# A causal way and a full way of attention behind one branch, and rope keys on all 128 rows

## The chip, the core and the metric

The kernel runs on one core of a Trainium2 chip. A core has a matmul engine (TensorE, "PE", with its weight loads as "PEld"), a vector engine (VectorE, "DVE"), an activation engine (ScalarE, "ACT"), GpSimd ("POOL") and SyncE ("SP"), each with an instruction stream of its own. They work on a memory on the chip, matmuls write into an accumulator memory (PSUM), and DMA queues move data from and to device memory. SyncE issues the weight loads, GpSimd most other transfers. The metric is the time of one execution on the device, in microseconds (us).

## What is computed

Three layers over 512 tokens of width 2048, all in fp32. The first is a recurrent mixer (two kinds of linear recurrence, a gate, an output projection, a layer norm). The second is an attention with 16 heads whose queries and keys are made from small inner vectors and have a part of 64 columns turned by position (rope). The third is an attention with 8 heads that subtracts two softmaxes from each other. The change touches only how the two attentions leave out what the mask forbids:

```python
CHUNK, Q_BLOCK, SEQ = 64, 128, 512

def chunk_allowed(pos_q, pos_k):
    return (pos_k // CHUNK)[:, None, :] <= (pos_q // CHUNK)[:, :, None]

def mla_attend(q, k, v, pos):          # second layer, 16 heads, d = 128 + 64
    ...
    sc = jnp.einsum('bhqd,bhkd->bhqk', qi, k_t).astype(jnp.float32) * scale
    sc = jnp.where(chunk_allowed(pi, pos)[:, None], sc, -jnp.inf)
    p = jax.nn.softmax(sc, axis=-1)
    return jnp.einsum('bhqk,bhkd->bhqd', p.astype(v_t.dtype), v_t)

def diff_attend(q, k, v, pos, lam):    # third layer, 8 heads, 2 components, value width 256
    ...
    sc = sc + bias[:, :, None]         # -slope * |distance|
    sc = jnp.where(chunk_allowed(pi, pos)[:, None, None], sc, -jnp.inf)
    p = jax.nn.softmax(sc, axis=-1)
    p_diff = p[:, :, 0] - lam * p[:, :, 1]
    return jnp.einsum('bhqk,bhkd->bhqd', p_diff.astype(v_t.dtype), v_t)

positions = jnp.arange(SEQ)            # an input of the kernel
```

The positions are an input. With positions that count up, a block of 128 queries sees its own block of keys and those before it, and nothing of the blocks behind.

## The kernel before

All activations lie transposed: 128 features on the partitions, 512 tokens along the free dimension. A matmul takes a weight block of 128 × 128 as its stationary operand and 512 columns (tokens) as the moving one. For accuracy each fp32 number is held as a high and a low part (`split`: ScalarE casts the high part, VectorE subtracts it to get the low part), and each product is three matmuls (`mm3`, lines 115 to 117: high × high, low × high, high × low) in a one-pass fp32 format. Weights come in units of 512 KB into three rotating tiles `raw`, and `unit` splits them into `whi` and `wlo`.

Each attention works head by head. `scores(j)` of the second layer makes, for each of 4 blocks `a` of 128 queries, a score tile of 128 × 512 with five matmuls: three for the 128 plain columns, two for the rope (line 572 with the key's high part on 128 rows, line 573 with its low part on the 64 rows of that head). `attention_rows` adds the mask (VectorE, line 316), takes the maximum, and ScalarE makes the exponentials; line 575 scales the rows by their sum. Then `PV` turns the 4 × 4 blocks (`turn`, line 609, one PE transpose each), splits them, and multiplies by the values (`step`). These pieces are hung into the gate's and the next pair's projections by slice number: `pv.at(7, 9, 12, 14)` means that the first turn stands ahead of slice 7 of a projection of 16 slices. The third layer does the same with `scores(a)` (two components, each with a bias tile `bm`) and two value halves.

A scheduler orders each engine's stream from this code; engines then wait for each other through semaphores.

At the start SyncE loads the first weight units and the input slices `f` in turn, ScalarE and VectorE split them, and TensorE begins with the two projections of `proj_side`.

Of the kernel before, what the change touches and what calls it, by code (L numbers as in the profile page):

```python
# [19 lines left out]
T = 512  # L20
# [7 lines left out]
class Core:  # L28
    def __init__(self, ctx, tc):
# [7 lines left out]
        self.hl = ent(tc.tile_pool(name="hl", bufs=1))  # L37
        self.ps = ent(tc.tile_pool(name="ps", bufs=2, space=PSUM))
        self.dr = ent(tc.tile_pool(name="dr", bufs=1, space=DRAM))
        self.ones = self.cp.tile([128, 128], F32, name="ones")  # L40
        nc.vector.memset(self.ones, 1.0)
        self.ones_r = self.cp.tile([128, 128], F32R, name="onesr")
        nc.vector.tensor_copy(self.ones_r, self.ones)
# [4 lines left out]
        self.consts = {}  # L48
        self.ahead = []


    def const_col(self, v):
        if v not in self.consts:
            t = self.cp.tile([128, 1], F32, name=f"c{len(self.consts)}")
            self.nc.vector.memset(t, float(v))
            self.consts[v] = t
        return self.consts[v]
# [35 lines left out]

    def unit(self, src, n):
# [3 lines left out]
        raw = self.wp.tile([128, 1024], F32, tag="raw", name="raw", bufs=3)  # L98
        self.nc.sync.dma_start(raw[:, :n], src)
# [60 lines left out]
    def hl_tiles(self, n=KD):  # L160
        h = [self.hl.tile([128, T], F32R, tag=f"h{i}", name=f"h{i}") for i in range(n)]
        l = [self.hl.tile([128, T], F32R, tag=f"l{i}", name=f"l{i}") for i in range(n)]
        return h, l

# [16 lines left out]
    def token_sums(self, wk, out, sq):  # L181
# [3 lines left out]
        d = wk.tile([128, 128], F32, tag="diag", name="diag", bufs=1)  # L185
        for a in range(4):
            self.nc.vector.tensor_tensor_reduce(out=d, in0=ps[:, a * 128:a * 128 + 128], in1=self.ident, scale=1.0,
                                                scalar=0.0, op0=ALU.mult, op1=ALU.add, accum_out=out[:, a:a + 1])
# [7 lines left out]
    def sigmoid(self, out, x, tmp):  # L196
# [3 lines left out]
        self.act(out, tmp, AF.Exp, scale=-1.0)  # L200

# [108 lines left out]
def attention_rows(co, wk, scores, bias, scale, nb):  # L310
# [3 lines left out]
    p = wk.tile([128, T], F32, tag="p", name="p", bufs=nb)  # L314
# [18 lines left out]
def mla_layer(co, w, tables, enter, after, out):  # L333
# [7 lines left out]
    with ExitStack() as ctx:  # L341
# [133 lines left out]
        for pr in range(8):  # L475
# [38 lines left out]
            kpl = wk.tile([128, T], F32R, tag="kpl", name="kpl", bufs=1)  # L514
# [8 lines left out]
            def k_rms(j):  # L523
# [12 lines left out]
                l = kpl[halves[j], :]  # L536
                co.tt(l, kpf[halves[j], :], h[halves[j], :].bitcast(F32), ALU.subtract)
# [27 lines left out]
            def scores(j):  # L565
                P = []
                hf = halves[j]
# [30 lines left out]
class PV:  # L598


    def __init__(self, co, wk, P, n, vh, vl, off):
# [3 lines left out]
    def turn(self, kt):  # L605
        co = self.co
        pt = co.psum("g")
        for a in range(4):
            co.nc.tensor.transpose(pt[:, a * 128:(a + 1) * 128], self.P[a][:, kt * 128:(kt + 1) * 128], co.ident)  # L609
        h = self.wk.tile([128, T], F32R, tag="pth", name="pth", bufs=2)  # L610
        l = self.wk.tile([128, T], F32R, tag="ptl", name="ptl", bufs=2)
        co.split(h, l, pt)
# [27 lines left out]
class Gated:  # L640
# [3 lines left out]
    def __init__(self, co, name, order=range(KD)):  # L644
# [3 lines left out]
        self.h, self.l = [None] * KD, [None] * KD  # L648

    def hl(self, i):  # L650
        co = self.co
        self.h[i] = co.hl.tile([128, T], F32R, tag=f"h{i}", name=f"h{i}")
        self.l[i] = co.hl.tile([128, T], F32R, tag=f"l{i}", name=f"l{i}")
# [9 lines left out]
    def get(self, first, eng=None):  # L663
# [4 lines left out]
        for u in range(KD // 2 - 1):  # L668
            raw = co.wp.tile([128, 1024], F32, tag="raw", name="raw", bufs=3)
# [1054 lines left out]
```

## Time and profile before

| | |
|---|---|
| Median of 3 runs | 3068.97 us (3066.61 to 3069.67) |
| The profiled execution | 3074.24 us |
| Its span, first to last instruction | 3072.5 us |
| Mean granted TensorE clock | 0.985 of full speed |
| Instructions | 43493 |
| Moved by DMA | 294.41 MB, 96 GB/s |

The profiled execution is a single one, 5.3 us above the median. A span is the time from the first instruction to the last. A matmul's shown duration contains its way through the engine, so the distance from one start to the next is what a matmul costs in a stream.

### The profile page before, as it was taken

Reading aid. Unit: us, or ns where it says so; the run is one execution under the profiler, and the core shown is the slowest. Engines: PE = TensorE matmul, PEld = TensorE weight load, DVE = VectorE, ACT = ScalarE, POOL = GpSimd, SP = SyncE. Lnnn points to the kernel's source line nnn. Section 1 sums busy time; section 2 is a strip of 40 time slices with the busy share of each in tenths; the row PEclk is TensorE's granted clock in tenths of the full one; section 3 lists DMA queues with packets and bytes.
Section 4 is the critical chain, followed back from the end, with each engine's and each line's share of the span. In section 5 each row is a group of like instructions: output and inputs, shape, how many; then the busy total and the mean of one; then the engine's idle time right before and its main releaser. Section 6 shows DMA issues by size and latency. Waiting matters only on the chain.

```text
span 3072.5 us, 43493 instructions
## 1 busy us (share of the span) xinstructions
PE 2995.8 (98%) x16606; PEld 2462.5 (80%) x16606; DVE 1841.7 (60%) x3617; ACT 1442.6 (47%) x2628; POOL 434.9 (14%) x793
## 2 busy tenths in 40 slices
PE   8799999999999899799999999999999999999999
PEld 6687787787787788577777787888888888888887
DVE  6455745647546585948777776346466556655632
ACT  5354545545545432646555665244444444444521
POOL 0312303303213310710000000100000000000000
PEclk9899999999999799899999999999999999999999
DMA  4222222223223343232221124432222222222443
GB/s 172 66 88 75 83 77 81 83 78 85 74 77 90 102 158 124 93 103 69 73 72 63 66 76 158 144 137 83 95 84 76 97 90 83 83 90 90 140 146 112
DMA packets 92033, 294.41 MB, mean 96 GB/s; under 512 B 15232, under 2 KB 15664, under 8 KB 91696
## 3 DMA queue, kind: packets, MB, share of 16 engines
q1 hardware_dynamic: 73984, 246.89, 23.5%
q0 software_dynamic: 17840, 44.74, 5.1%
q8 instruction: 130, 2.13, 0.3%
q14 instruction: 79, 0.65, 0.1%
HBM read 263.95 MB, written 27.53 MB: 95 GB/s over the span
## 4 chain that ended last, share of the span: by engine, by line
PE 62%; DVE 2%; ACT 1%; DMA 1%; issue 1%; POOL 0%; DVEq 0%; ACTq 0%; SPq 0%
PE pj L115 17%; PE pj L117 17%; PE pj L116 17%; PE g L115 2%; PE g L116 2%; PE g L117 2%; PE g L609 1%; PE g L573 1%; PE g L194 1%; PE g L193 1%; PE g L572 0%; DVE t L76 0%; DVE l L73 0%; DVE wlo L73 0%; DMA raw<-og 0%
## 5 line engine op out<-in xcount | busy, mean ns | idle before, releaser
L115 PE MATMUL pj<-h,whi 128*128 128x512 f32 x2848 | 1145.4, 402 | 15.0 <-ACT h L81 14.2
L116 PE MATMUL pj<-l,whi 128*128 128x512 f32 x2848 | 1119.4, 393 | 9.8 <-DVE l L73 9.2
L117 PE MATMUL pj<-h,wlo 128*128 128x512 f32 x2848 | 1119.5, 393 | 4.7 <-DVE wlo L73 4.6
L73 DVE TENSOR_TENSOR wlo<-raw,whi 128x512 fp32r<-128x512 f32 x864 | 601.0, 699 | 767.7 <-ACT whi L81 740.6
L81 ACT CAST whi<-raw 128x512 fp32r<-128x512 f32 x864 | 534.0, 620 | 924.2 <-PE pj L116 778.7
L115 PEld LDWEIGHTS pj<-h,whi 128*128 128x128 f32 x2848 | 538.4, 189 | 137.6 <-ACT h L81 15.9
L117 PEld LDWEIGHTS pj<-h,wlo 128*128 128x128 f32 x2848 | 538.8, 189 | 123.5 <-DVE wlo L73 6.9
L116 PEld LDWEIGHTS pj<-l,whi 128*128 128x128 f32 x2848 | 539.7, 189 | 116.2 <-DVE l L73 11.8
L115 PE MATMUL pj<-whi,h 128*128 128x256 f32 x768 | 221.3, 288 | 0.0
L116 PE MATMUL pj<-wlo,h 128*128 128x256 f32 x768 | 217.2, 283 | 0.0
L117 PE MATMUL pj<-whi,l 128*128 128x256 f32 x768 | 217.1, 283 | 0.0
L115 PEld LDWEIGHTS pj<-whi,h 128*128 128x128 f32 x768 | 147.0, 191 | 4.7 <-issue 1.4
L116 PEld LDWEIGHTS pj<-wlo,h 128*128 128x128 f32 x768 | 147.2, 192 | 1.2
L117 PEld LDWEIGHTS pj<-whi,l 128*128 128x128 f32 x768 | 147.1, 192 | 0.2
L70 ACT ACTIVATE p<-p,mx,rq 128x512 f32<-128x512 f32 x128 | 104.2, 814 | 84.1 <-DVE mx L318 83.7
L73 POOL TENSOR_TENSOR gs<-gs,rs 128x512 f32<-128x512 f32 x16 | 20.4, 1291 | 712.3 <-ACT rs L70 712.3
L73 POOL TENSOR_TENSOR mt<-m,at 128x60 f32<-128x60 f32 (+24 forms) x248 | 93.3, 376 | 92.6 <-DMA at<-d 73.8
L73 POOL TENSOR_TENSOR m<-m,mt 128x60 f32<-128x60 f32 (+24 forms) x248 | 95.4, 385 | 19.4
L73 DVE TENSOR_TENSOR ptl<-g,pth 128x512 fp32r<-128x512 f32 x96 | 65.3, 686 | 52.9 <-ACT pth L81 52.7
L73 DVE TENSOR_TENSOR sql<-sq,sqh 128x512 fp32r<-128x512 f32 x96 | 66.3, 691 | 32.7 <-ACT sqh L81 32.5
L81 ACT CAST pth<-g 128x512 fp32r<-128x512 f32 x96 | 56.2, 586 | 63.2 <-PE g L609 58.5
L81 ACT CAST sqh<-sq 128x512 fp32r<-128x512 f32 x96 | 59.4, 618 | 18.0 <-DVE sq L73 8.9
(440 smaller groups left out, 4015.5 us busy)
## 6 DMA issues: line engine op xcount, KB each, us to landing
raw<-w_in SPq DMA_DIRECT2D x114, 512.0 KB, 3.2
raw<-b_qk SPq DMA_DIRECT2D x64, 512.0 KB, 3.2
raw<-a_in SPq DMA_DIRECT2D x50, 512.0 KB, 3.2
raw<-w_out SPq DMA_DIRECT2D x32, 512.0 KB, 3.3
raw<-a_out SPq DMA_DIRECT2D x32, 512.0 KB, 3.6
raw<-b_v SPq DMA_DIRECT2D x32, 512.0 KB, 3.2
raw<-b_g SPq DMA_DIRECT2D x32, 512.0 KB, 3.2
raw<-b_out SPq DMA_DIRECT2D x32, 512.0 KB, 3.4
```

Source lines behind the costliest of these rows:

```text
L70: self.nc.scalar.activation(out, in_, func, scale=scale, **kw)
L73: return (eng or self.nc.vector).tensor_tensor(out, in0=a, in1=b, op=op)
L81: self.nc.scalar.copy(hi, src)
L115: mm(out, lhsT=ahi, rhs=bhi, start=start, stop=False)
L116: mm(out, lhsT=ahi, rhs=blo, start=False, stop=False)
L117: mm(out, lhsT=alo, rhs=bhi, start=False, stop=stop)
L193: self.nc.tensor.matmul(out, lhsT=ones, rhs=h, start=True, stop=False)
L194: self.nc.tensor.matmul(out, lhsT=ones, rhs=l, start=False, stop=True)
L573: mm(sc, lhsT=qps[j][hf, ts], rhs=kps[j][1], start=False, stop=True)
L609: co.nc.tensor.transpose(pt[:, a * 128:(a + 1) * 128], self.P[a][:, kt * 128:(kt + 1) * 128], co.ident)
```

## The change

The program asks once, on the device, whether every block of 128 positions lies wholly behind the block before it (in chunks of 64), and then runs one of two complete copies of all three layers. In the first copy (`co.causal`), a score tile for query block `a` has only the first 128·(a+1) keys, the turns leave out the blocks above the diagonal, and a value product for key block `kt` covers only the queries from 128·kt on. The second copy computes everything, as before. In both copies the low part of the rope key has 128 rows. Buffers that were handed out by a pool are now fixed tiles, so that both copies use the same ones; the constants are columns of one tile, and the diagonal of the token sums is written back to PSUM in place.

```diff
+        self.raws = [self.wp.tile([128, 1024], F32, name=f"raw{i}", bufs=1) for i in range(3)]
+        self.causal = False
+
+    def span(self, a):
+
+        return a * 128 + 128 if self.causal else T
...
+    def load(self, src):
+
+        if self.loaded:
+            return self.loaded.pop(0)
+        raw = self.raws.pop(0)
+        self.raws.append(raw)
...
+def in_order(co, wk, w):
...
+    row = wk.tile([1, T], I32, name="posrow1")
+    f = row.bitcast(F32)
+    nc.sync.dma_start(row, w["pos"].rearrange("(a t) -> a t", a=1))
+    dve.tensor_scalar(row, row, 6, None, op0=ALU.arith_shift_right)
+    dve.tensor_copy(f, row)
+    hi = wk.tile([1, 8], F32, name="order")
+    lo, flag = hi[:, 4:8], co.cp.tile([1, 1], I32, name="inorder")
+    fb = f.rearrange("p (a t) -> p a t", a=4)
+    dve.tensor_reduce(hi[:, 0:4], fb, axis=AX.X, op=ALU.max)
+    dve.tensor_reduce(lo, fb, axis=AX.X, op=ALU.min)
+    for a in (2, 1):
+        co.tt(lo[:, a:a + 1], lo[:, a:a + 1], lo[:, a + 1:a + 2], ALU.min)
+    co.tt(hi[:, 0:3], lo[:, 1:4], hi[:, 0:3], ALU.is_gt)
+    dve.tensor_reduce(hi[:, 3:4], hi[:, 0:3], axis=AX.X, op=ALU.min)
+    dve.tensor_copy(flag, hi[:, 3:4])
+    return flag
...
-    p = wk.tile([128, T], F32, tag="p", name="p", bufs=nb)
+    p = wk.tile([128, T], F32, tag="p", name="p", bufs=nb)[:, 0:n]
...
-                l = kpl[halves[j], :]
-                co.tt(l, kpf[halves[j], :], h[halves[j], :].bitcast(F32), ALU.subtract)
+                l = wk.tile([128, T], F32R, tag="kpl", name="kpl")
+                co.tt(l, kpf, h.bitcast(F32), ALU.subtract)
...
-                    sc = co.psum("g")
+                    n = co.span(a)
+                    sc = co.psum("g")[:, 0:n]
                     ts = slice(a * 128, a * 128 + 128)
-                    co.mm3(sc, qs[j][0][:, ts], qs[j][1][:, ts], ks[j][0], ks[j][1], True, False)
-                    mm(sc, lhsT=qps[j][:, ts], rhs=kps[j][0], start=False, stop=False)
-                    mm(sc, lhsT=qps[j][hf, ts], rhs=kps[j][1], start=False, stop=True)
-                    p, rs = attention_rows(co, wk, sc, mask[:, a, :], rq[:, j, a:a + 1], 4)
+                    co.mm3(sc, qs[j][0][:, ts], qs[j][1][:, ts], ks[j][0][:, 0:n], ks[j][1][:, 0:n], True, False)
+                    mm(sc, lhsT=qps[j][:, ts], rhs=kps[j][0][:, 0:n], start=False, stop=False)
+                    mm(sc, lhsT=qps[j][:, ts], rhs=kps[j][1][:, 0:n], start=False, stop=True)
+                    p, rs = attention_rows(co, wk, sc, mask[:, a, 0:n], rq[:, j, a:a + 1], 4, n)
...
-        for a in range(4):
+        a0 = kt if co.causal else 0
+        for a in range(a0, 4):
...
+            o = o[:, kt * 128 if self.co.causal else 0:T]
...
+        with tc.tile_pool(name="ord", bufs=1) as wk:
+            ordered = nc.values_load(in_order(co, wk, w), min_val=0, max_val=1)
+        first = [co.load(x) for x in (w["w_in"][32, 0], w["xT"][0:256].rearrange("(a p) t -> p a t", p=128),
+                                      w["w_in"][8, 0])]
+        consts = dict(co.consts)
+
+        with tc.If(ordered > 0) as cmp:
+            co.causal, co.loaded = True, list(first)
+            layers(co, w, out)
+        with cmp.Else():
+            co.causal, co.consts, co.loaded = False, consts, list(first)
+            layers(co, w, out)
```

The third layer's `scores` gets the same `n` for its bias tile, its three matmuls and its softmax.

TensorE, in the middle of the second layer, where the scores of an odd head begin. Names read out<-moving,stationary: `g` is the PSUM score tile, `knh`/`knl` the key's parts, `qnh`/`qnl` the query's, `kph`/`kpl` the rope key's, `qps` the rope query's. Before, the first two of four query blocks:

```order
L115 MATMUL g<-knh,qnh 128x512
L116 MATMUL g<-knl,qnh 128x512
L117 MATMUL g<-knh,qnl 128x512
L572 MATMUL g<-kph,qps_12325 128x512
L573 MATMUL g<-kpl,qps_12325 128x512
L115 MATMUL g<-knh,qnh 128x512
L116 MATMUL g<-knl,qnh 128x512
L117 MATMUL g<-knh,qnl 128x512
L572 MATMUL g<-kph,qps_12325 128x512
L573 MATMUL g<-kpl,qps_12325 128x512
```

The same place in the first copy after:

```order
L136 MATMUL g<-knh,qnh 128x128
L137 MATMUL g<-knl,qnh 128x128
L138 MATMUL g<-knh,qnl 128x128
L610 MATMUL g<-kph,qps_12098 128x128
L611 MATMUL g<-kpl,qps_12098 128x128
L136 MATMUL g<-knh,qnh 128x256
L137 MATMUL g<-knl,qnh 128x256
L138 MATMUL g<-knh,qnl 128x256
L610 MATMUL g<-kph,qps_12098 128x256
L611 MATMUL g<-kpl,qps_12098 128x256
```

The order is the same and the widths are cut; the third and fourth block have 384 and 512 columns.

TensorE, the end of a gate projection of the second layer, where the last turn and the last value products of a head stand (`p` is a softmax row tile, `ident` the identity, `pth`/`ptl` the turned parts, `vh`/`vl` the values). Before:

```order
L609 MATMUL g<-ident,p 128x128 x4
L115 MATMUL pj<-h_11273,whi 128x512
L116 MATMUL pj<-l_11289,whi 128x512
L117 MATMUL pj<-h_11273,wlo 128x512
L115 MATMUL pj<-h_11274,whi 128x512
L116 MATMUL pj<-l_11290,whi 128x512
L117 MATMUL pj<-h_11274,wlo 128x512
L115 MATMUL g<-pth,vh 128x512
L116 MATMUL g<-ptl,vh 128x512
L117 MATMUL g<-pth,vl 128x512
L115 MATMUL g<-pth,vh 128x512
```

After:

```order
L649 MATMUL g<-ident,p 128x128
L136 MATMUL pj<-h_79,whi 128x512
L137 MATMUL pj<-l_95,whi 128x512
L138 MATMUL pj<-h_79,wlo 128x512
L136 MATMUL pj<-h_80,whi 128x512
L137 MATMUL pj<-l_96,whi 128x512
L138 MATMUL pj<-h_80,wlo 128x512
L136 MATMUL g<-pth,vh 128x256
L137 MATMUL g<-ptl,vh 128x256
L138 MATMUL g<-pth,vl 128x256
L136 MATMUL g<-pth,vh 128x128
```

Three of the four last transposes are gone, and the products of the last two key blocks have 256 and 128 columns.

SyncE, at the program's start (`raw` is a weight unit or, after, also the first input slice; `f` the other input slices). Before:

```order
L99 DMA raw<-w_in 128x1024
L728 DMA f<-xT 128x2x512
L99 DMA raw<-w_in 128x1024
L728 DMA f<-xT 128x2x512 x3
L99 DMA raw<-w_in 128x1024
```

After:

```order
L226 DMA posrow_114<-pos 1x512
L113 DMA raw_108<-w_in 128x1024
L111 DMA raw_109<-xT 128x2x512
L113 DMA raw_110<-w_in 128x1024
L740 TENSOR_LOAD inorder
L740 ISA x2
L745 COMPARE_AND_BRANCH
L783 DMA f<-xT 128x2x512 x3
L113 DMA raw_108<-w_in 128x1024
```

The position load stands first, and the reading of the flag and the branch stand between the third big load and the fourth.

## Rows read from the trace of the kernel before

**Rows 1.** The page, part 1: busy time, share of span, instructions.

```profile
PE 2995.8 (98%) x16606; PEld 2462.5 (80%) x16606; DVE 1841.7 (60%) x3617; ACT 1442.6 (47%) x2628; POOL 434.9 (14%) x793
```

**Rows 2.** Busy time by stretch: from:to, length, then engines; clock, DMA share, GB/s.

```profile
36.00:1036.00 1000.00, 959.40 (x6645) 783.23 (x6643) 567.42 (x1007) 487.81 (x886) 260.48 (x582) 0.96 0.26 81
...
1395.00:1900.00 505.00, 504.59 (x2393) 394.55 (x2392) 388.89 (x924) 303.98 (x578) 28.91 (x32) 1.00 0.24 80
...
2180.00:2890.00 710.00, 710.00 (x3809) 613.84 (x3809) 415.97 (x906) 321.50 (x596) 21.68 (x24) 1.00 0.26 90
```

**Rows 3.** Waits: engine and line, whom it waited for, total us, times, longest.

```profile
ACT whi L81 <- PE pj L116: 778.7, 517, 3.1
...
PE g L1334 <- DVE pm L1330: 26.3, 2, 16.9
```

**Rows 4.** Timeline of TensorE, scores of an even head: start, duration, instruction.

```profile
1529.06 0.39 PE L117 MATMUL g<-knh,qnl 128*128 128x512 f32 x1
1529.29 0.40 PE L572 MATMUL g<-kph,qps 128*128 128x512 f32 x1
1529.62 0.50 PE L573 MATMUL g<-kpl,qps 64*128 64x512 f32 x1
1530.05 0.50 PE L115 MATMUL g<-knh,qnh 128*128 128x512 f32 x1
...
1531.60 0.50 PE L115 MATMUL g<-knh,qnh 128*128 128x512 f32 x1
```

**Rows 5.** Timeline of TensorE, matmuls of 256 columns; five lie between.

```profile
1397.77 0.28 PE L115 MATMUL pj<-whi,ckvh 128*128 128x256 f32 x1
...
1398.46 0.28 PE L115 MATMUL pj<-whi,ckvh 128*128 128x256 f32 x1
```

**Rows 6.** Groups by line and form on TensorE: xcount, busy us, mean ns.

```profile
L609 PE MATMUL g<-ident,p 128*128 128x128 f32 x384 | 57.7, 272 | 0.0
...
L573 PE MATMUL g<-kpl,qps 64*128 64x512 f32 x64 | 31.7, 496 | 0.0
```

**Rows 7.** Timeline of TensorE, the first turns of the same head.

```profile
1540.11 0.60 PE L609 MATMUL g<-ident,p 128*128 128x128 f32 x4
...
1540.78 0.40 PE L116 MATMUL pj<-l,whi 128*128 128x512 f32 x1
```

**Rows 8.** Timeline of TensorE, eight passes of 64 columns, one matmul of 512 between.

```profile
207.74 1.00 PE L1521 MATMUL g<-x 128*128 128x64 f32 x8
...
208.86 0.40 PE L116 MATMUL pj<-l,whi 128*128 128x512 f32 x1
```

**Rows 9.** Timeline of TensorE, four plain fp32 matmuls in eight passes, likewise.

```profile
204.77 1.06 PE L1510 MATMUL g<-q,k 128*128 128x128 f32 x8
...
205.90 0.39 PE L116 MATMUL pj<-l,whi 128*128 128x512 f32 x1
```

**Rows 10.** Timeline of the start, ScalarE and TensorE, with the idle time before.

```profile
4.57 1.14 ACT L81 CAST whi<-raw 128x512 fp32r<-128x512 f32 x2 [2.47 <-DMA raw<-w_in]
...
6.52 0.80 PE L115 MATMUL pj<-h,whi 128*128 128x512 f32 x1 [6.52 <-ACT h L81]
...
10.28 0.63 PE L115 MATMUL pj<-h,whi 128*128 128x512 f32 x1
...
10.71 0.63 PE L116 MATMUL pj<-l,whi 128*128 128x512 f32 x1
```

**Rows 11.** DMA issues: count, KB each, median us from issue to landing.

```profile
raw<-w_in SPq DMA_DIRECT2D x114, 512.0 KB, 3.2
...
dcols<-cols_b POOLq DMA_DIRECT2D x1, 4.0 KB, 1.8
```

**Rows 12.** Groups on VectorE, 1395 to 1900 us: xcount, busy us, mean ns, idle before.

```profile
L73 DVE TENSOR_TENSOR wlo<-raw,whi 128x512 fp32r<-128x512 f32 x116 | 79.5, 688 | 39.7 <-ACT whi L81 39.5
...
L320 DVE RECIPROCAL mx<-mx 128x1 f32<-128x1 f32 x64 | 10.0, 157 | 4.1 <-ACT p L70 4.1
```

**Rows 13.** Timeline of VectorE, the last softmax row of the same head.

```profile
1537.83 0.49 DVE L575 TENSOR_SCALAR p<-p,mx 128x512 f32<-128x512 f32 x1
```

More of the change, by code (lines that the diff above doesn't have):

```diff
@@ L36, in __init__ @@
         self.wp = ent(tc.tile_pool(name="wp", bufs=3))
-        self.hl = ent(tc.tile_pool(name="hl", bufs=1))
+        hl = ent(tc.tile_pool(name="hl", bufs=1))
+        self.h = [hl.tile([128, T], F32R, name=f"h{i}") for i in range(KD)]
+        self.l = [hl.tile([128, T], F32R, name=f"l{i}") for i in range(KD)]
         self.ps = ent(tc.tile_pool(name="ps", bufs=2, space=PSUM))
         self.dr = ent(tc.tile_pool(name="dr", bufs=1, space=DRAM))
-        self.ones = self.cp.tile([128, 128], F32, name="ones")
+        self.ones_r = self.cp.tile([128, 128], F32R, name="onesr")
+        self.ones = self.ones_r.bitcast(F32)
         nc.vector.memset(self.ones, 1.0)
-        self.ones_r = self.cp.tile([128, 128], F32R, name="onesr")
-        nc.vector.tensor_copy(self.ones_r, self.ones)
         self.ident = self.cp.tile([128, 128], F32, name="ident")
@@ L48, in __init__ @@
         self.consts = {}
+        self.columns = self.cp.tile([128, 32], F32, name="columns")
         self.ahead = []
+        self.loaded = []
+        self.raws = [self.wp.tile([128, 1024], F32, name=f"raw{i}", bufs=1) for i in range(3)]
+        self.causal = False
+    def span(self, a):
+        return a * 128 + 128 if self.causal else T
     def const_col(self, v):
         if v not in self.consts:
-            t = self.cp.tile([128, 1], F32, name=f"c{len(self.consts)}")
+            n = len(self.consts)
+            t = self.columns[:, n:n + 1]
             self.nc.vector.memset(t, float(v))
@@ L91, in rsqrt @@
         self.act(out, tmp, AF.Exp, scale=-0.5)
+    def load(self, src):
[3 more added lines that the diff above has]
+        self.raws.append(raw)
+        if len(src.shape) == 3:
+            self.nc.sync.dma_start(raw.rearrange("p (a t) -> p a t", a=2), src)
+        else:
+            self.nc.sync.dma_start(raw[:, :src.shape[1]], src)
+        return raw
     def unit(self, src, n):
@@ L97, in unit @@
             return self.ahead.pop(0)
-        raw = self.wp.tile([128, 1024], F32, tag="raw", name="raw", bufs=3)
-        self.nc.sync.dma_start(raw[:, :n], src)
+        raw = self.load(src)
         parts = []
@@ L158, in proj_side @@
                     self.mm3(o, *self.cut(p, j * 128), xh[k], xl[k], k == 0, k == KD - 1)
[L160 to L163, printed above, removed]
     def psum(self, tag):
@@ L200, in sigmoid @@
         self.act(out, tmp, AF.Exp, scale=-1.0)
+def in_order(co, wk, w):
+    nc = co.nc
+    dve = nc.vector
+    row = wk.tile([1, T], I32, name="posrow1")
[14 more added lines that the diff above has]
+    return flag
 def positions_part(co, tmp, cp, w, maskd, distd, trigd):
@@ L307, in positions_part, with attention_rows @@
     yield
-def attention_rows(co, wk, scores, bias, scale, nb):
+def attention_rows(co, wk, scores, bias, scale, nb, n):
     nc = co.nc
-    p = wk.tile([128, T], F32, tag="p", name="p", bufs=nb)
+    p = wk.tile([128, T], F32, tag="p", name="p", bufs=nb)[:, 0:n]
     mx = wk.tile([128, 4], F32, tag="mx", name="mx", bufs=4)
@@ L668, in get @@
         for u in range(KD // 2 - 1):
-            raw = co.wp.tile([128, 1024], F32, tag="raw", name="raw", bufs=3)
-            co.nc.sync.dma_start(raw.rearrange("p (a t) -> p a t", a=2), src[u])
+            raw = co.load(src[u])
             for a in range(2):
@@ L701, in program, with layers @@
         nc = tc.nc
+        with tc.tile_pool(name="ord", bufs=1) as wk:
[9 more added lines that the diff above has]
+            layers(co, w, out)
+def layers(co, w, out):
+    tc, nc = co.tc, co.nc
+    with ExitStack() as ctx:
         dve = nc.vector
@@ L726, in enter1 @@
                         ahead.append(co.unit(w["w_in"][32, u // 4], 1024))
-                    f = wk.tile([128, 2, T], F32, tag="f", name="f")
-                    nc.sync.dma_start(f, src[u])
+                    if u:
+                        f = wk.tile([128, 2, T], F32, tag="f", name="f")
+                        nc.sync.dma_start(f, src[u])
+                    else:
+                        f = co.load(src[u]).rearrange("p (a t) -> p a t", a=2)
                     if u % 4 == 0:
```

33 lines of the change are left out of this document (15 added, 18 removed).

## The prediction

> **What bounds the kernel now.** I read the page's busy shares first, then the stages, then the waits of TensorE, then single matmuls in order of time. TensorE is busy for 98% of the span, no other engine for more than 60% [rows 1]. By stage, the two attentions (1395 to 1900 us and 2180 to 2890 us) show it busy all the time at the full granted clock, with VectorE at 77% (388.9 of 505 us) and ScalarE at 60% in the first of them [rows 2]. ScalarE waits 778.7 us for TensorE to give weight tiles back; TensorE's own longest wait, 16.9 us, lies in the first layer's triangle work, which the change leaves alone [rows 3]. So a microsecond of TensorE's stream in an attention is a microsecond of the kernel, as long as nobody else comes late.
>
> A busy TensorE is not one at its peak, so prices are taken from the distance between starts. A matmul of 512 moving columns is followed 0.23 us later (1529.06 to 1529.29) [rows 4]; six with 256 columns take 0.69 us, 0.115 each [rows 5].
>
> **The narrow blocks.** I call "a set" one kind of matmul over the four blocks of a head. Before it is four times 512 columns, 4 × 0.23 = 0.92 us; after it has 128, 256, 384 and 512. In the first attention a head has 5 kinds of score matmul and 3 of values: 16 × 8 = 128 sets. In the second it has 2 components × 3 scores and 2 halves × 3 values: 8 × 12 = 96. Together 224 sets; the rope matmul's count of 64 is 16 heads × 4 blocks [rows 6].
>
> Of the new widths only 256 has a row with these operands: 0.115 us. For 384 I take 0.17, between its neighbours by columns. For 128 the rows give ends far apart. By columns it would be half of 0.115, so 0.057. But a matmul brings weights of its own, 128 × 128: four turns of 128 columns and the matmul behind them take 0.67 us (1540.11 to 1540.78), less 0.23 that is 0.44, 0.11 each [rows 7]; eight passes of only 64 columns take 1.12 − 0.23 = 0.89 us, 0.11 each again [rows 8]. Half the columns, same price: the weights set it, and a 128-column score has the same weights. The upper end is a plain fp32 matmul of 128 columns, run as two passes: eight passes take 1.13 − 0.23 = 0.90 us, so 0.22 for a pair [rows 9]. I take 0.11, since the weight load is what these rows share with the new matmul. A set then costs 0.11 + 0.115 + 0.17 + 0.23 = 0.625 us and gives 0.295; 224 sets give **66.1 us**. With 0.057 it would be 78.0, with 0.22 it would be 41.4.
>
> The Trainium skill, "TensorE: Matmul & The Clock Gate", section "LDWEIGHTS (loading the stationary operand)", counts a load's columns divided by 1.2 as its ns, 107 for 128 columns, and speaks against gains below 256 columns here; the rows agree (0.11). The same page's isolated gap for 128 columns is about 56 ns; by that estimate the sets would give 78 us.
>
> **The turns.** Of 16 transposes a head keeps 10, in 24 heads (384 now [rows 6]): 144 × 0.11 = **15.8 us**.
>
> **The rope matmul.** The low part of the key's rope gets 128 rows instead of 64. Before, a block of five score matmuls takes 1.55 us (1530.05 to 1531.60) where five streaming ones would take 5 × 0.23 = 1.15. The extra stands around the 64-row matmul: its forerunner takes 0.33, it takes 0.43 (1529.29, 1529.62, 1530.05) [rows 4]. With all rows it is a matmul like its neighbours: 64 × 0.40 = **25.6 us**, counted before the columns are cut. VectorE's subtraction for it keeps 512 columns, and so its cost.
>
> The gains are 66.1 + 15.8 + 25.6 = 107.5 us. VectorE and ScalarE lose the same columns in softmax and splits; they wait for TensorE there, so that counts nothing.
>
> **The start.** SyncE now loads the positions first, and every engine reads the flag and branches before its real work. Three big loads are issued ahead of the branch, the rest behind it. Today ScalarE's first cast starts at 4.57 and TensorE at 6.52 us [rows 10]. After: a small load at the head of the queue lands 1.8 us behind its issue at best [rows 11], so near 3 us. Four VectorE steps over 512 columns at up to 0.69 and five tiny ones at 0.16 [rows 12] make up to 3.6; I take 3.2, so 6.2. The register load and the branch have no row: at least nothing, at most a big load's 3.2 us [rows 11]; I take 2, nearest to a small load's 1.8. ScalarE then starts near 8.2, and five casts (two take 1.14 us [rows 10]), 2.8 us, now stand ahead of the first matmul: 11.0 instead of 6.52, 4.5 us late. A held-back load lands 3.2 us after 8.2, at 11.4; the two slices loaded ahead keep TensorE 12 × 0.43 = 5.2 us, as matmuls follow each other 0.43 us apart in the first microseconds (10.28 to 10.71 [rows 10]). So nothing more is lost. **+4.5 us**, bounds 1 (the loads are the bound anyway) and 10.
>
> The Trainium skill, "Runtime: NRT & Kernel Launch", section "Instruction fetch mechanics", warns that a taken branch whose target is not yet fetched stalls for a fetch. No row here shows that; it speaks for the upper end.
>
> **The end.** Each engine jumps over the other way. No row; between nothing and 3.2 us of a load [rows 11]. I take the middle, **+1.5 us**.
>
> **New waits.** In an even head the first turn follows the last softmax row closely: VectorE's last row starts at 1537.83 and takes 0.49 [rows 13], the turn starts at 1540.11 [rows 7], 1.8 us behind. The scores ahead shrink from 4 × 1.55 = 6.2 to 5 × 0.625 = 3.1 us, so the turn comes 3.1 us earlier. The softmax shortens too, with 1280 of 2048 columns, but the gate's sigmoid ahead of it does not. If its end came no earlier than before, each even head would wait 1.3 us, 8 × 1.3 = 10.4; if it follows by 1.3 or more, none. VectorE starts on the narrow blocks sooner and has 768 columns less, so I put **+2 us**, bounds 0 and 10.4. The second attention has its turns eight slices of a projection behind the last scores, which stay 512 wide.
>
> **Sum.** −107.5 + 4.5 + 1.5 + 2 = −99.5 us. The profiled execution took 3074.24 us (its span of 3072.5 and 1.7 around it), so 2974.7; the median of the runs shown, 3068.97, lies 5.3 us below it, so 2969.5, said as **2970 us**.
>
> **Rivals.**
> - *Narrow matmuls cost like fp32 ones* (0.22 us for 128 columns). For it: no row has this operand type below 256 columns. Against: at 256 the price is exactly half of that at 512. The sets give 41.4 instead of 66.1: 2994 us. Chance 0.18.
> - *The turns wait for the softmax*, the full 10.4 us, and the value matmuls for their narrower splits by as much again: 2970 − 2 + 20.8 = 2988 us. VectorE at 77% speaks for it, its waits for TensorE against. Chance 0.09.
> - *The other way is taken* because the flag comes out 0. Then only the rope's 25.6 us remains, less 6 for start and end: 3049 us. The positions count up, so the smallest chunk of each block is above the block before it: against. Chance 0.02.
> - *Slower: the clock.* At the low level of 1.2 GHz a 512-column matmul takes 0.43 us instead of 0.23 at 2.4 [rows 4, 10]. If TensorE fell idle at every head, the granted clock could fall as in the first layer, where it has its long waits (0.96 there, 1.00 in the attentions [rows 2]). Work that takes 0.23 loses 0.20; the gain of 99.5 is eaten when 114 us of full-speed work run at the low level, near 5 us in each of 24 heads. At 7 us a head it is 146 lost, 3116 us. Today's attentions have no wait near that. Chance 0.03.
>
> **How the numbers follow.** The forecast has 0.66, the rivals 0.32, and 0.02 is for a gain that goes elsewhere. About 0.2% (6 us) is what a measurement of this kernel tells from none. All but the clock (0.03) and that last 0.02 are faster: 0.95 faster, 0.02 the same, 0.03 slower. The range goes from the cheap 128-column price with the start at its lower bound (2970 − 12 − 4 = 2954, said as 2953) to the dear one with the start and the waits well up in their bounds (2994 + 9 = 3003); the other way and the clock lie outside.
>
> **What would show it.** In the profile after: score matmuls 0.11, 0.115, 0.17 and 0.23 us apart, no gap around the rope pair, 240 turns, a first matmul near 11 us. The first attention's 505 us should become 431 (128 sets, 96 turns and the rope: 74), the second lose 34. The forecast is wrong if 128 columns take 0.2, if TensorE waits for VectorE's rows ahead of turns, or if the start takes over 15 us.

## The result and the profile after

The changed kernel takes 2982.09 us (median of 4 runs, 2971.75 to 2985.1) where the kernel before takes 3069.32 us; the ratio is 0.9704, 95% interval 0.9683 to 0.9725. The profiled execution took 2985.1 us, its span is 2983.1 us, 89.4 less than the 3072.5 of before. The forecast was 2970 us, 12 us too low; the measured time lies inside its range of 2953 to 3003 us. First the page's busy times (as in [rows 1]) and the same three stretches as in [rows 2], at the times where they lie now (from:to, length, PE, PEld, DVE, ACT and POOL busy; clock, DMA share, GB/s):

```profile
PE 2892.7 (97%) x16462; PEld 2416.9 (81%) x16462; DVE 1782.5 (60%) x3625; ACT 1400.3 (47%) x2628; POOL 433.4 (15%) x793
```

```profile
40.00:1040.00 1000.00, 959.11 (x6653) 782.74 (x6653) 566.85 (x1009) 487.32 (x885) 258.92 (x582) 0.96 0.27 80
...
1410.00:1850.00 440.00, 430.46 (x2261) 364.47 (x2260) 352.20 (x887) 267.06 (x559) 30.11 (x34) 1.00 0.29 92
...
2120.00:2800.00 680.00, 680.00 (x3757) 594.61 (x3756) 385.25 (x905) 310.21 (x596) 21.69 (x24) 1.00 0.28 92
```

The first layer is as it was. The second attention is shorter and TensorE has no idle time in it. In the first attention TensorE is idle for 9.5 of 440 us, where it had 0.4 of 505. Its waits (engine and line, whom it waited for, total us, times, longest) show by whom:

```profile
PE g L1393 <- DVE pm L1389: 26.4, 2, 16.2
...
PE g L137 <- DVE ptl L83: 5.8, 7, 0.8
...
PE g L649 <- DVE p L613: 1.9, 1, 1.9
```

The first line is the triangle work of the first layer, with a wait of 16.2 us at 115 us of the span and one of 10.3 us at 997; before it was 16.9 and 9.4. The second and third line are new: seven value products wait for the low part of a turned block, and one turn for a softmax row. The scores of a head, which took 4 × 1.55 us [rows 4], now look like this (TensorE's timeline: start, duration, instruction):

```profile
1532.45 0.28 PE L136 MATMUL g<-knh,qnh 128*128 128x128 f32 x1
1532.57 0.28 PE L137 MATMUL g<-knl,qnh 128*128 128x128 f32 x1
...
1532.79 0.27 PE L610 MATMUL g<-kph,qps 128*128 128x128 f32 x1
1532.90 0.28 PE L611 MATMUL g<-kpl,qps 128*128 128x128 f32 x1
1533.02 0.33 PE L136 MATMUL g<-knh,qnh 128*128 128x256 f32 x1
...
1533.42 0.28 PE L610 MATMUL g<-kph,qps 128*128 128x256 f32 x1
1533.54 0.28 PE L611 MATMUL g<-kpl,qps 128*128 128x256 f32 x1
...
1534.00 0.34 PE L138 MATMUL g<-knh,qnl 128*128 128x384 f32 x1
1534.17 0.34 PE L610 MATMUL g<-kph,qps 128*128 128x384 f32 x1
...
1535.67 0.39 PE L136 MATMUL pj<-cqh,whi 128*128 128x512 f32 x1
```

From start to start: 0.11 us at 128 columns, 0.12 at 256, 0.17 at 384, no gap around the rope pair, and 3.22 us for the 20 matmuls (1532.45 to 1535.67) where 5 × 0.625 = 3.13 was forecast.

The start, against [rows 10] (timeline, DVE, SP, ACT and PE in turn, with the idle time before):

```profile
2.14 0.41 DVE L227 TENSOR_SCALAR posrow<-posrow 1x512 int32<-1x512 int32 x1 [0.91 <-DMA posrow<-pos]
...
5.06 0.14 DVE L238 CAST inorder<-order 1x1 int32<-1x1 f32 x1
...
6.17 1.41 SPq L783 DMA_DIRECT2D f<-xT  x3
...
5.85 1.14 ACT L91 CAST whi<-raw 128x512 fp32r<-128x512 f32 x2 [3.75 <-DVE inorder L238]
...
9.44 1.19 PE L136 MATMUL pj<-h,whi 128*128 128x512 f32 x2 [9.44 <-ACT h L91]
```

The flag is written at 5.20 us, ScalarE works again 0.65 us later. The first matmul starts 2.9 us later than before (9.44 against 6.52), but its inputs are then nearer, and 1.9 us are left from the 60th projection matmul on.

To set kernels beside each other I take the start times of the same projection matmuls (`pj`, 11712 of them in every kernel, counted from 0): first attention from number 4810 to 7000, second from 7400 to 11000, and a "triangle stretch" in the first layer from 3450 to 3550, which holds the second of the two waits of line 1393 (8.2 to 10.7 us long in the 14 profiles). That stretch takes 62 to 77 us in the 14 profiles, whatever the kernel, so I also give the span without it. The columns of stages come from one profiled execution each; a ratio refers to runs of the kernel before from the same set. All times in us:

| kernel | median (runs) | ratio to before, 95% | first att. | second att. | triangle | span less triangle |
|---|---|---|---|---|---|---|
| before | 3069.32 (4) | 1 | 647.1 | 786.4 | 75.6 | 2996.9 |
| changed | 2982.09 (4) | 0.9704 (0.9683 to 0.9725) | 586.3 | 753.9 | 76.8 | 2906.3 |
| after_again | 2972.3 (5) | 0.9686 (0.9661 to 0.9710) | 585.6 | 755.7 | 63.4 | 2906.9 |
| no_branch | 2974.91 (4) | 0.9685 (0.9659 to 0.9711) | 585.9 | 753.4 | 77.1 | 2903.7 |
| other_way | 3052.24 (9) | 0.9937 (0.9918 to 0.9956) | 621.3 | 787.2 | 70.8 | 2975.8 |
| rope_64_rows | 2996.63 (5) | 0.9761 (0.9736 to 0.9786) | 597.7 | 754.1 | 63.8 | 2916.4 |
| scores_256 | 2968.53 (4) | 0.9680 (0.9649 to 0.9711) | 579.5 | 754.1 | 62.2 | 2894.7 |
| rope_late | 2977.59 (4) | 0.9689 (0.9661 to 0.9717) | 584.9 | 753.9 | 76.3 | 2903.8 |
| gate_on_vector | 2978.53 (4) | 0.9708 (0.9678 to 0.9738) | 582.8 | 753.6 | 75.3 | 2899.2 |
| row_on_scalar | 2973.02 (4) | 0.9678 (0.9645 to 0.9712) | 577.9 | 753.9 | 75.6 | 2895.5 |
| row_on_scalar_again | 2971.42 (5) | 0.9678 (0.9656 to 0.9701) | 577.5 | 754.1 | 71.8 | 2894.7 |
| last_head_late | 2985.15 (4) | 0.9719 (0.9683 to 0.9755) | 588.4 | 754.0 | 76.2 | 2907.0 |
| row_scalar_low_pool | 2975.38 (5) | 0.9685 (0.9663 to 0.9707) | 578.1 | 754.0 | 74.1 | 2899.6 |
| row_scalar_low_pool_late | 2963.86 (4) | 0.9655 (0.9632 to 0.9679) | 579.0 | 753.9 | 62.7 | 2899.6 |

### The profile page after: what moved, and what is told of

The parts are those of the page before. It is cut to its first block, busy times and chain, and to the rows that moved or that the text cites. A ratio compares the mean times of both kernels' runs of the same rounds, so it can differ in the third digit from the quotient of the medians.

```text
span 2983.1 us, 43252 instructions
## 1 busy us (share of the span) xinstructions
PE 2892.7 (97%) x16462; PEld 2416.9 (81%) x16462; DVE 1782.5 (60%) x3625; ACT 1400.3 (47%) x2628; POOL 433.4 (15%) x793
## 4 chain that ended last, share of the span: by engine, by line
PE 56%; DVE 5%; ACT 2%; issue 1%; DMA 1%; POOL 0%; DVEq 0%; POOLq 0%; ACTq 0%
PE pj L138 17%; PE pj L136 17%; PE pj L137 17%; PE g L137 1%; PE g L138 1%; PE g L136 1%; DVE rt L83 1%; PE g L210 1%; PE g L649 1%; DVE l L83 1%; PE g L209 1%; ACT sg L80 1%; DVE p L613 0%; DVE t L86 0%; DMA raw<-og 0%
## 5 line engine op out<-in xcount | busy, mean ns | idle before, releaser
L80 ACT ACTIVATE p<-p,mx,rq 128x128 f32<-128x128 f32 (+3 forms) x128 | 83.1, 650 | 62.6 <-DVE mx L357 62.3
L83 DVE TENSOR_TENSOR ptl<-g,pth 128x512 fp32r<-128x512 f32 (+1 forms) x96 | 45.9, 486 | 39.0 <-ACT pth L91 39.0
L80 ACT ACTIVATE rs<-rs 128x512 f32<-128x512 f32 x80 | 50.5, 631 | 31.8 <-DVE rs L86 21.2
```

Source lines behind the costliest of these rows:

```text
L80: self.nc.scalar.activation(out, in_, func, scale=scale, **kw)
L83: return (eng or self.nc.vector).tensor_tensor(out, in0=a, in1=b, op=op)
```

## The experiments

**What the branch costs.** `no_branch` keeps the first copy alone:

```diff
-            ordered = nc.values_load(in_order(co, wk, w), min_val=0, max_val=1)
-        with tc.If(ordered > 0) as cmp:
-            co.causal, co.loaded = True, list(first)
-            layers(co, w, out)
-        with cmp.Else():
-            co.causal, co.consts, co.loaded = False, consts, list(first)
-            layers(co, w, out)
+        co.causal, co.loaded = True, list(first)
+        layers(co, w, out)
```

> The first copy alone: the position load, the flag and the branch are left out, and so is the second copy; everything else is as in the changed kernel. Theory (the flag and the branch cost the start and the jump costs the end): the first matmul returns from 9.4 to about 6.5 us, the lag of 1.9 us that is left of it after the first slices goes, and the tail behind the last matmul falls from 6.0 to 4.0 us, so the span is 3.9 us shorter than the changed kernel's, with the two attentions unchanged. Rival (the lag comes from the new order of loads and the fixed tiles, which stay here): less than 1 us changes.

The first matmul is back at 6.51 us, a lead of 2.0 us over the changed kernel stays behind the first slices, and from the last matmul to the end of the span it is 4.0 us instead of 6.1. Both attentions are as in the changed kernel within 0.5 us. So the branch costs 2.0 us at the start and 2.0 at the end; the span shows less of it (2.3), as the first layer's stages took 2.6 us more in this profile.

**The other way.** `other_way` turns the comparison round, so that the second copy runs:

```diff
-    co.tt(hi[:, 0:3], lo[:, 1:4], hi[:, 0:3], ALU.is_gt)
+    co.tt(hi[:, 0:3], lo[:, 1:4], hi[:, 0:3], ALU.is_lt)
```

> The comparison in the test of the order is turned round (is_lt), so the flag comes out 0 and the second copy runs: full blocks, all turns, every value product over all queries, with the rope key's low part on 128 rows. Nothing is left out. It is the rope part alone, plus the branch: minus 25.6 us in the first attention and plus 3.9 us at start and end give 21.7 us less than the kernel before, near 3051 us. Rival (the branch's far side is dearer, since its code is fetched from behind the first copy): the first matmul comes later than 9.5 us. If the waits for ptl at odd heads come from the faster rope matmuls and not from the narrow blocks, they show here too (the excess of the first attention above 8 us).

The time is what the theory gave (3052 us, 3051 said), and the first attention is 647.1 − 621.3 = 25.8 us shorter than before: the rope part, alone. None of the seven waits is there, so the faster rope alone does not make them; they need the narrow blocks. At the start the timeline (ACT, SP, DVE, PE) shows the rival too:

```profile
9.87 2.17 ACT L91 CAST whi<-raw 128x512 fp32r<-128x512 f32 x4 [7.77 <-issue]
...
10.04 2.34 SPq L783 DMA_DIRECT2D f<-xT  x3
...
10.06 1.03 DVE L1148 MEMSET rs<- 128x512 bf16 x2 [4.82 <-issue]
...
12.62 0.80 PE L136 MATMUL pj<-h,whi 128*128 128x512 f32 x1 [12.62 <-ACT h L91]
```

Three engines come back 4.0 us later (9.87 against 5.85, 10.04 against 6.17, 10.06 against 6.09) after the same flag at the same time: jumping to the far copy costs 4 us more than falling through to the near one. The Trainium skill, "Runtime: NRT & Kernel Launch", section "Instruction fetch mechanics", says that a taken branch to code not yet fetched stalls for it; these 4.0 us and the 2.0 us at the near copy's end, where it jumps over the other, agree. That the time goes into fetching was not measured by itself.

**Rope rows.** `rope_64_rows` takes the low part's 64 extra rows back, in the narrow blocks:

```diff
-                l = wk.tile([128, T], F32R, tag="kpl", name="kpl")
-                co.tt(l, kpf, h.bitcast(F32), ALU.subtract)
+                l = wk.tile([128, T], F32R, tag="kpl", name="kpl")[halves[j], :]
+                co.tt(l, kpf[halves[j], :], h[halves[j], :].bitcast(F32), ALU.subtract)
...
-                    mm(sc, lhsT=qps[j][:, ts], rhs=kps[j][1][:, 0:n], start=False, stop=True)
+                    mm(sc, lhsT=qps[j][halves[j], ts], rhs=kps[j][1][:, 0:n], start=False, stop=True)
```

> Only the rope part of the change is undone: the low part of the rope key has the 64 rows of its head again, in the narrow blocks. Theory A (each change of the number of rows costs a fixed 0.40 us, whatever the columns): 64 times 0.40 = 25.6 us more than the changed kernel, nearly 3008 us, all in the first attention, and the same extra around a 64-row matmul of 128 columns as around one of 512. Theory B (the extra is paid per column): 320 of 512 columns on the mean, 16 us more. If neither, and VectorE's shorter subtraction (64 rows) shortens its queue, the wait for ptl at odd heads is shorter than 1.04 us.

TensorE's timeline, the end of a 128-column block and the next one's first matmuls:

```profile
1503.84 0.27 PE L610 MATMUL g<-kph,qps 128*128 128x128 f32 x1
1504.04 0.32 PE L611 MATMUL g<-kpl,qps 64*128 64x128 f32 x1
1504.30 0.38 PE L136 MATMUL g<-knh,qnh 128*128 128x256 f32 x1
1504.52 0.28 PE L137 MATMUL g<-knl,qnh 128*128 128x256 f32 x1
```

The forerunner takes 0.20, the 64-row matmul 0.26, the next one 0.22, where the changed kernel has 0.11, 0.12 and 0.17. Over the medians of 16 heads the extra of the three is 0.29 us at 128 columns and 0.39, 0.40, 0.40 at 256, 384, 512: it belongs to the change of rows, not to the columns (theory A, a little too dear at 128). They sum to 23.7 us; only 11.4 come out (597.7 against 586.3), since with this slower stream the seven waits are gone and 0.6 us is left at the last head.

**The price by weights.** `scores_256` makes the narrowest score block twice as wide:

```diff
-        return a * 128 + 128 if self.causal else T
+        return max(a * 128 + 128, 256) if self.causal else T
```

> A score block has at least 256 columns, so the first query block of each head is 256 wide instead of 128 in both attentions (80 + 48 = 128 score matmuls; the mask still covers the added keys). Theory (the weights set the price, 0.110 at 128 and 0.119 at 256 columns): 128 times 0.009 = 1.2 us more, within the scatter. Rival (columns set it): 128 times 0.06 = 7.7 us more. A further loss at the odd heads would say that VectorE and ScalarE, which get 128 columns more per head, are the bound of the first attention by now.

The second attention is 0.2 us longer for 48 such matmuls (0.4 by the theory, 2.9 by the rival), and the score matmuls of the first attention take 0.7 us more in sum for 80 (0.7 and 4.8), so columns do not set the price at 128. That the weights do is seen in the first layer of the changed kernel, where eight passes of 64 columns (fp32, two passes to a matmul) have 128 weight columns in one place and 64 in another:

```profile
208.87 1.01 PE L1580 MATMUL g<-x 128*128 128x64 f32 x8
...
481.55 0.68 PE L1590 MATMUL g<-x 128*64 128x64 f32 x8
```

At full clock, from start to start, the first stand 0.112 us apart and the second 0.058 (medians): half the weight columns, half the price. The first attention is 6.8 us *shorter*, and its seven waits are gone. Neither theory had that. It led me to what VectorE does in the changed kernel at an odd head (timeline of POOL, DVE, ACT and PE in turn):

```profile
1536.15 1.29 POOL L83 TENSOR_TENSOR gs<-gs,sg 128x512 f32<-128x512 f32 x1 [1.04 <-ACT sg L80]
...
1536.12 1.41 DVE L613 TENSOR_SCALAR p<-p,mx 128x128 f32<-128x128 f32 x1
...
1538.24 0.35 DVE L613 TENSOR_SCALAR p<-p,mx 128x256 f32<-128x256 f32 x1
...
1541.35 2.77 DVE L83 TENSOR_TENSOR rt<-qp,sin 32x512 f32<-32x512 f32 x4 [0.29 <-ACT qp L523]
...
1546.63 1.14 DVE L83 TENSOR_TENSOR ptl<-g,pth 128x512 fp32r<-128x512 f32 x2
...
1545.40 0.58 ACT L91 CAST pth<-g 128x512 fp32r<-128x512 f32 x1
...
1546.09 0.45 PE L136 MATMUL g<-pth,vh 128*128 128x512 f32 x1
1547.36 0.50 PE L137 MATMUL g<-ptl,vh 128*128 128x512 f32 x1 [0.82 <-DVE ptl L83]
```

Scaling the narrowest softmax row takes 1.41 us, four times what the row of twice its width takes (0.35). GpSimd multiplies the gate in just that time. All seven odd heads with a pair behind them show the same two. (At seven even heads the row of 256 columns runs into that head's multiplication, which has begun 0.7 us earlier, and takes 0.72 us instead of 0.35; nothing waits there.) VectorE then goes on late through the next pair's rope to the split `ptl`, and the value product stands 1.04 us longer than a normal 0.23, the one behind it 0.11 longer: 1.15 us a head. Before, no scaling met that multiplication; in `scores_256` the first two rows of such a head are ready after it and take 0.61 us together:

```profile
1515.07 0.61 DVE L613 TENSOR_SCALAR p<-p,mx 128x256 f32<-128x256 f32 x2
```

**Order or lateness.** `rope_late`, planned before I saw this, moves the rope, and the split into `qps` behind it, to after the odd head's second turn:

```diff
-            rope(wk, qp, qp)
...
...
             finish([1])
+            rope(wk, qp, qp)
```

> The changed kernel with one thing moved: the turning of the next pair's queries by position (rope, on VectorE) and the split behind it stand in the code after the second turn of the odd head instead of before the first. Nothing is left out. Theory (VectorE's queue: the split of the turned block stands behind the rope there): the seven waits of 1.04 us of the first value product for ptl go, 7.3 us less, the last head's two waits (4.1 us) stay. Rival (ScalarE's cast pth is late of itself, behind sqh, or the softmax is): the waits stay, 0 us. Third: the wait goes and comes back at the scores of the next pair, which need the turned queries: 0 us, with a wait at line 610.

The waits for `ptl` are gone, but as many stand a little later, at the token sums (1.15 us longer than normal each), as the waits show:

```profile
PE g L210 <- DVE sql L83: 7.2, 8, 1.0
```

So the order within VectorE's queue only chooses who waits (the third outcome, at another place than I named): the queue itself is over 1 us late.

**Who makes it late.** Two edits part GpSimd from that row, `gate_on_vector` by moving the multiplication (first lines), `row_on_scalar` by moving the row:

```diff
-            co.tt(gs, gs, sg, ALU.mult, nc.gpsimd)
+            co.tt(gs, gs, sg, ALU.mult)
...
-                    nc.vector.tensor_scalar(p, p, rs, None, op0=ALU.mult)
+                    if a:
+                        nc.vector.tensor_scalar(p, p, rs, None, op0=ALU.mult)
+                    else:
+                        nc.scalar.activation(p, p, AF.Identity, scale=rs)
```

> The changed kernel with one thing moved: the last multiplication of the gate (gs times sg, 128 x 512) runs on VectorE instead of GpSimd. Nothing is left out. Theory (the scaling of the first softmax row of an odd head takes 1.41 us instead of 0.28 because it meets GpSimd's multiplication of 1.29 us, and this lateness is the wait of 1.04 us): the scaling takes 0.28 us, VectorE spends 0.69 us on the multiplication in the same place, so its queue is 0.44 us earlier and each of the seven waits falls from 1.04 to 0.6 us: 3 us less in the first attention, no POOL work beside it. Rival (VectorE's queue is too long as such, GpSimd has no part): the queue gets 0.69 us longer, the waits grow to 1.7 us: 5 us more.

> The changed kernel with one thing moved: the first softmax row block of each head of the first attention (128 x 128) is scaled by ScalarE instead of VectorE. Nothing is left out. Theory (VectorE is held up by GpSimd's multiplication at this one instruction): VectorE gets rid of 1.41 us ahead of the turning of the queries, ScalarE has 0.48 us more; the seven waits for ptl go, 7.3 us less in the first attention. Rival (it is ScalarE's chain of exponentials, squares and casts that is late): the waits grow by 0.48 us each, 3.4 us more. Third: another VectorE instruction of the same kind (the maximum's scaling of 128 x 1) meets GpSimd's multiplication in its place and the waits stay.

With the multiplication on VectorE the row takes 0.28 us again, and the value product's excess falls from 1.04 to 0.60 us (start to start 0.83):

```profile
1529.73 0.69 DVE L83 TENSOR_TENSOR gs<-gs,sg 128x512 f32<-128x512 f32 x1
1530.33 0.28 DVE L613 TENSOR_SCALAR p<-p,mx 128x128 f32<-128x128 f32 x1
...
1539.69 0.40 PE L136 MATMUL g<-pth,vh 128*128 128x512 f32 x1
1540.52 0.50 PE L137 MATMUL g<-ptl,vh 128*128 128x512 f32 x1 [0.43 <-DVE ptl L83]
```

VectorE has more work there and is earlier: 3.5 us less in the first attention, as the theory said, against the rival's 5 more. With the row on ScalarE nothing waits (ACT, then PE):

```profile
1529.85 0.39 ACT L616 ACTIVATE p<-p,mx 128x128 f32<-128x128 f32 x1
...
1539.96 0.40 PE L136 MATMUL g<-pth,vh 128*128 128x512 f32 x1
1540.19 0.39 PE L137 MATMUL g<-ptl,vh 128*128 128x512 f32 x1
```

All seven waits are gone (7 × 1.15 = 8.1 us), 8.4 us less in the first attention. Being held is not enough by itself: in `rope_64_rows` the same row takes 1.39 us at these seven heads too and no value product waits, since TensorE comes to it 11.5 us after the row's start (1526.31 to 1537.79) instead of 10.0. It takes the held row and the shorter stream together. The Trainium skill, "SBUF — State Buffer", section "Who interferes with whom", says that VectorE and GpSimd share a pair of ports and that one of the two is blocked for the whole of the other's instruction, `tensor_scalar` being a kind that can need the pair; the rows agree (1.41 us beside GpSimd's 1.29, 0.28 without). It gives the pair to whoever issues first; that the rows bear out only in part. VectorE's record begins 0.03 us before GpSimd's (1536.12 against 1536.15) and VectorE is held; at seven other heads, in `scores_256`, it begins 0.15 us before, takes its 0.35 us, and GpSimd's multiplication takes 1.35 us.

**The last head.** In the changed kernel its first turn stands 2.1 us for a softmax row, and 7 us later a weight tile is 2.0 us late by DMA. `last_head_late` hangs that head's work further back:

```diff
-            for i in range(5):
+            for i in range(25):
                 yield
-                finish([i])
+                if i in (9, 13, 17, 21, 24):
+                    finish([(9, 13, 17, 21, 24).index(i)])
...
-        bt.add(last(), 4)
+        bt.add(last(), 1)
```

> The changed kernel with the last head's turns and value products hung later into the output projection: its first turn at the 10th slice instead of the 8th, the others three or four slices apart behind it. Nothing is left out. Theory (the last head's first turn waits 2.1 us for its last softmax row, which is as late as before while the stream ahead of it has become shorter): the wait of 2.1 us goes; the second stall of 2.0 us, where a weight tile comes late by DMA, stays: 2 us less in all. Rival (both stalls are one delay of the weight tiles, which are read at the pace of VectorE): the second stall takes over what the first gives up, 0 us. The seven waits at odd heads stay at 1.04 us in both.

The rival held for the stalls: one of 3.6 us stands in place of two (4.1 together). That the first attention is 2.1 us longer neither had said. It is the clock: behind the longer stall TensorE was at 0.53 of full speed from 1831 to 1838 us, and 14 matmuls from 1831.84 us on take 5.99 us, which at 0.23 each would be 3.2. In the changed kernel the granted clock stays at 1.00 there. The next version asks whether VectorE paces those tiles, on top of `row_on_scalar`, and a third adds the later turns to it:

```diff
-        mla_layer(co, w, tables, enter2, gates[1].put, lambda bt: begin(1, "a_out", bt.tick, bt.drain))
+        mla_layer(co, w, tables, enter2, gates[1].put, lambda bt: begin(1, "a_out", bt.tick, bt.drain, nc.gpsimd))
```

> Two things on top of the changed kernel: the first softmax row block is scaled by ScalarE (as in the run before), and the low parts of the gated heads for the second output projection are made by GpSimd instead of VectorE. Nothing is left out. Theory (at the last head VectorE paces both the last rows and the weight tiles, since it makes the low parts in between): the stalls of 1.4, 0.95 and 0.5 us there and the 1.8 us that eight matmuls at the low clock cost behind them go, up to 4.6 us less than with the row alone; 573 to 575 us between the marks instead of 577.9, 13 us under the changed kernel in the whole. Rival (GpSimd's subtractions of 1.3 us each hold up VectorE's instructions that need the same way into the memory): stalls at the last head grow, 578 us or more.

> As the version with ScalarE's row and GpSimd's low parts, and the last head's first turn at the 10th slice of the output projection instead of the 8th. Theory (with the tiles no longer paced by VectorE, the later turn takes away what wait is left of the last softmax row): up to 2 us less than without, if there is a wait left there. Rival (as with the later turns alone: the last slices' value products then crowd at the end): 0 to 2 us more.

No gain: 578.1 and 579.0 against 577.9, as the rivals said. In the first of the two the low clock behind the last head's stalls, which `row_on_scalar` has for 3.4 us, is gone, but ahead of them two value products now stand 0.73 and 0.82 us longer than normal. VectorE now meets GpSimd's subtractions (timeline of `row_scalar_low_pool`, DVE, then POOL):

```profile
1798.78 1.51 DVE L83 TENSOR_TENSOR knl<-kf,knh 128x512 fp32r<-128x512 f32 x1 [0.19 <-ACT knh L91]
1800.22 1.78 DVE L83 TENSOR_TENSOR kpl<-kpf,kph 128x512 fp32r<-128x512 f32 x1
1801.92 0.68 DVE L83 TENSOR_TENSOR ptl<-g,pth 128x512 fp32r<-128x512 f32 x1
...
1796.75 6.38 POOL L83 TENSOR_TENSOR l<-raw,h 128x512 fp32r<-128x512 f32 x4 [2.10 <-ACT h L91]
```

A subtraction with both inputs in the memory on the chip takes 1.51 and 1.78 us instead of 0.68; `ptl`, with one input in PSUM, takes its 0.68. GpSimd has a part in the changed kernel's last head too: beside its multiplication one of VectorE's subtractions takes 1.75 us (at 1821.42), and in `gate_on_vector` the stalls there come to 2.4 us instead of 4.1. What would free the last head altogether stays open. The lowest median of the table, 2963.86 us of the last version, goes back, as far as its profile shows, to the triangle stretch (62.7 us) and not to the edit.

**Again, for the time.** The changed kernel and the best version once more:

> The changed kernel as it is, for a time on the same chip and in the same call as the two versions below. It should give the 586.3 us between the same two projections of the first attention as in its first profile, seven waits of 1.04 us and one pair at the last head; its time scatters by what the triangle stretch of the first layer takes (62 to 77 us in the profiles so far).

> The version with the first row block scaled by ScalarE once more, in more rounds. Between the marks of the first attention it should take 577.9 us again (8.4 less than the changed kernel), and its time should lie 8 us below the changed kernel's: 2972 to 2974 us when the triangle stretch of the first layer takes its 75 us, near 2961 when it takes 63; ratio to before 0.965 to 0.969.

The stages repeat within 0.7 us (first attention) and 1.8 us (second). Over both sets of nine runs the median is 2979.49 us for the changed kernel and 2973.00 us for `row_on_scalar`; the intervals of their ratios overlap, as the triangle stretch alone moves a run by up to 15 us. The gain of 8 us in the first attention stands in both pairs of profiles (586.3 and 585.6 against 577.9 and 577.5); in the totals it is not clear of the scatter. `row_on_scalar` is the version I would keep, with `scores_256` as its equal (span less triangle 2895.5 and 2894.7 us against 2894.7).

## Why the prediction was right, and where its size was off

**The bound.** Right: the attentions gave the time, 60.8 us (647.1 − 586.3) and 32.5 us (786.4 − 753.9).

**Narrow blocks, turns.** Right: 128 columns cost 0.11 us, and the dear rival (0.22) is out. The second attention, which has only these two terms, gave 32.5 of 33.6 us (30.7 in its second profile). The 384 and the first 256 columns behind a narrower block are a little dearer than said (0.17 and 0.16 in the rows; 3.22 against 3.13 us a head).

**Rope.** Right: 25.8 us shown alone, 25.6 said.

**New waits.** This is the step that failed, in place and size. I bounded it by the even heads' first turns, at most 10.4 us, and took 2. Those turns never waited. The waits came at the odd heads (seven of 1.15 us, 8.1 in all) and at the last head (2.1 and 2.0 us, where before had 0.6): 11.6 us, 9.6 more than said and past the bound. I had followed ScalarE's and VectorE's work in length, and had not set GpSimd's multiplication beside VectorE's rows, which now come earlier and land on it. The rival of late softmax priced 20.8 us of waits; its second half, value matmuls late by their splits, is what came, but from another cause.

**Start and end.** The start was over-priced: the test's nine VectorE steps end at 5.20 us (6.2 said), reading the flag and branching takes 0.65 us (2 said), and 1.9 us remain of 4.5. The end costs 2.0 (1.5 said).

**The sum.** Against −99.5 us the span gave −89.4: 9.6 lost by the waits, 1.1 by the second attention and 0.5 by the end, less 2.6 won back by the start. The 1.6 that are left lie in the first attention (74 said, less 11.6 of waits, is 62.4; it gave 60.8); 1.5 of them are the 0.1 us by which each of the 16 heads' scores is dearer than said. So part of the closeness was luck: the start, priced too high, hid a part of the waits. That the medians lie 87 us apart and not 89 is within the scatter of the triangle stretch.

## What to carry to other kernels

A matmul that carries its own 128 weight columns has a floor, here 0.11 us: cutting its moving side below 256 columns gave next to nothing more (0.12 to 0.11), so price narrow blocks by the floor and look for gain in whole instructions left out. When the bound engine gets faster, lay out anew which instructions of VectorE and GpSimd now run at the same time, not only how long each queue is: one row of 128 columns, held for 1.1 us in each of seven heads, cost seven stalls. And a wait that disappears when its instruction is moved may only have moved to the next consumer; look for it there before calling it solved.

## What the runs showed of the hardware

The scatter between runs lies mainly in one place. Behind the second wait of the triangle work, 8 to 11 us long, TensorE was at 0.50 of full speed, 1.2 GHz, for a time that differs between executions of like code, and of the same code. Windows of the changed kernel, where TensorE is idle for 10.6 of the first 20 us:

```profile
990.00:1000.00 10.00, 6.63 (x49) 4.89 (x45) 5.18 (x12) 6.66 (x13) 4.71 (x7) 1.00 0.45 68
1000.00:1010.00 10.00, 2.76 (x37) 2.73 (x38) 5.45 (x8) 0.58 (x1) 4.37 (x5) 0.51 0.27 92
...
1030.00:1040.00 10.00, 10.00 (x54) 7.89 (x56) 5.03 (x8) 1.76 (x3) 3.67 (x3) 0.50 0.54 164
1040.00:1050.00 10.00, 9.27 (x116) 7.19 (x113) 3.00 (x3) 6.47 (x15) 5.31 (x4) 0.94 0.36 113
```

and of `scores_256`, at the same work, where it is idle for 8.2 of the first 20 us:

```profile
990.00:1000.00 10.00, 1.92 (x9) 1.26 (x7) 5.43 (x9) 4.11 (x8) 4.37 (x5) 0.71 0.37 54
1000.00:1010.00 10.00, 9.87 (x119) 9.01 (x121) 7.18 (x16) 5.59 (x11) 2.68 (x2) 0.78 0.28 97
1010.00:1020.00 10.00, 10.00 (x98) 7.95 (x94) 9.74 (x19) 6.29 (x14) 6.97 (x5) 1.00 0.42 113
```

In the first TensorE works at the low level until about 1040 us, in the second it is back at full speed by 1010; the stretch takes 76.8 and 62.2 us. The second profile of the changed kernel, `after_again`, is of the short kind (63.4 us). Over the 14 profiles the stretch takes 62 to 64 us where the low level lasts 10 us, 71 to 72 where it lasts 31, and 74 to 77 where it lasts 37 to 41. The length of the wait ahead does not settle it: waits of 8.5 to 8.9 us stand ahead of 10, 31, 37 and 41 us alike. What decides it was not tried. Whoever measures a change of under 15 us in this kernel should compare stages, not totals.
